# Attention stage of a two-layer diffusion step: TensorE in written order, 18 output products moved into its end

## The chip, the cores and the metric

The kernel runs on one core of a Trainium2 chip. The metric is device time in microseconds (us) of one execution; lower is better. Five engines work side by side and meet only at semaphores: PE (TensorE, matrix products; PEld is its weight load), DVE (VectorE), ACT (ScalarE), POOL (GpSimd) and SP (SyncE, which here only issues transfers). Each engine takes its instructions strictly in the order in which they stand in its queue. An instruction whose data is not there holds up everything behind it on that engine.

## The reference, cut to what matters

Layer 0 is gated grouped-query attention, layer 1 a bidirectional gated recurrence. There are 512 latent tokens and 128 context tokens, width 1024, 16 query heads over 4 key/value heads of 64. Context tokens see only context; latent tokens see context and latent.

```python
h = x * (1.0 + sc) + sh                       # sh, sc, g: three parts of silu(cond) @ ada_w[i] + ada_b[i]
q, k, v, gt = split(h @ w_in)                 # layer 0
q, k = rope(rms_norm(q)), rope(rms_norm(k))
o = softmax(q @ k.T / 8.0) @ v
out = (o * silu(gt)) @ w_out
x = layer_norm(ALPHA * x + g * out)           # then layer 1, of the same frame
```

Everything is float32. Most products are made of three float32r products: each operand is cut into a high and a low part, and high*high, high*low and low*high are summed.

## The kernel before, in words

Tokens go in five tiles of 128 (`TT = 5`: four latent, one context). Layer 0 runs in three stretches: a lead-in (modulation, keys, values, gate, the query heads of group 0), the attention weave, and the output projection with its layer norm (`Norm`, `out_mms`) followed by the transposition for layer 1 (`h1_tile`). Layer 1 fills the second half of the time and its code is not touched.

**The weave.** Two generators take turns. `att_gen` walks over nine units for each key/value group c = 0..3: eight `sample_unit` (one head, 256 latent queries) and one `prompt_unit`. A unit has fronts (scores `sc` in a two-bank PSUM tile, row maximum `nm` on DVE, exponential on ACT, scaling of `p` by POOL) and backs (transposes `pt` of the probabilities, evacuation to `pts` by ACT or DVE); a pair of units ends with the product with the values (`pot`, for the context unit `pscp`, `ptp`, `potp`). Fronts run two units ahead. `Side` hands out everything else, 0.62 of a step (`SIDE_B`) for each step of the attention: the query products `qmm` and their transposes `qps` for the next group (`q_gen`), the modulation products of layer 1 (`ada_gen`, PSUM tile `adaps`), and at the end the weights of the output projection (`wo_gen`) and the split of the gated result (`split_gs`).

**The ring of raw weights.** Every weight block (512 KB) is loaded by SP into one of three `raw` tiles (`rawp`, bufs 3), in the fixed order of the list `order`; `pump` writes the next load when fewer than two (`RAW_AHEAD = 2`) are waiting. A load can start only when the block three places earlier has been used up. Around the attention the list reads: two `attn_w_in` blocks for group c, eight `ada_s` blocks k0..k7, two `attn_w_in` blocks for group c+1, eight more, ...; after the fourth eight come eight `attn_w_out` blocks. An `ada_s` block is used up by four products on PE (`ada_mms` does two blocks at a call: eight products). A block of `attn_w_in` or `attn_w_out` is used up when ACT has cast it (`whi`, `wohi`) and DVE has subtracted (`wlo`, `wolo`).

**What sets the order.** Everything up to the output projection is traced inside `first_half = tc.block(schedule_with_timeline_sim=True)`. There a planner lays out each engine's queue by a timeline of its own: an instruction moves ahead of others of its engine when the planner's timeline says that it is ready sooner. An instruction given to `keep_in_program_order` (`pin`) stays behind the one traced before it on its engine. Loads on SP are pinned; before the change few PE instructions of the attention are.

**PSUM.** The attention has three one-bank tiles (`pt`, `qmm`, `adaps` and others in turn), two two-bank tiles (`sc`, `pscp`) and one bank for `pot`. The output projection opens a new set of four two-bank tiles (`Phase(4, 0)`).

## Time and profile before

| | |
|---|---|
| median of 3 runs | 845.33 us (842.23 to 845.51) |
| the profiled execution: its time | 845.58 us |
| its span, first to last instruction | 843.5 us |
| mean granted TensorE clock | 0.988 of full |
| PE busy | 816.5 us of the span |
| attention weave | from about 140 to 337 us |
| output projection | from 337.0 us |

The span is cut by engine; times in the profile count from the first instruction. A line such as L276 is a line of the kernel before. A chain row gives start, length and what ran; a wait row gives the total, the number of times and the longest. Operations on plain float32 operands show twice as many PE records as products are written: `x16` in the trace is eight `adaps` products.

### The profile page before, as it was taken

Reading aid. Unit: us, or ns where it says so; the run is one execution under the profiler, and the core shown is the slowest. Engines: PE = TensorE matmul, PEld = TensorE weight load, DVE = VectorE, ACT = ScalarE, POOL = GpSimd, SP = SyncE. Lnnn points to the kernel's source line nnn. Section 1 sums busy time; section 2 is a strip of 40 time slices with the busy share of each in tenths; the row PEclk is TensorE's granted clock in tenths of the full one; section 3 lists DMA queues with packets and bytes.
Section 4 is the critical chain, followed back from the end, with each engine's and each line's share of the span. In section 5 each row is a group of like instructions: output and inputs, shape, how many; then the busy total and the mean of one; then the engine's idle time right before and its main releaser. Section 6 shows DMA issues by size and latency. Waiting matters only on the chain.

```text
span 843.5 us, 19410 instructions
## 1 busy us (share of the span) xinstructions
PE 816.5 (97%) x8157; PEld 732.1 (87%) x8157; DVE 532.1 (63%) x954; ACT 380.3 (45%) x769; POOL 213.6 (25%) x263
## 2 busy tenths in 40 slices
PE   8999999989999998999999999999999999999994
PEld 6789999768888766888999999999999999998774
DVE  3675534665557666776438575767668575858476
ACT  2242535563556767222434534435434544445232
POOL 0123001535334743010001304143333314121121
PEclk8999999999999999999999999999999999999997
DMA  9923120145141245630323322331332323314041
GB/s 330 387 86 105 55 72 26 52 162 196 51 157 52 100 133 169 225 125 35 111 66 67 108 68 82 83 108 52 107 89 83 93 67 89 120 65 157 26 157 75
DMA packets 34134, 92.50 MB, mean 110 GB/s; under 512 B 5040, under 2 KB 12224, under 8 KB 34048
## 3 DMA queue, kind: packets, MB, share of 16 engines
q1 hardware_dynamic: 23280, 73.05, 25.9%
q0 software_dynamic: 4864, 14.44, 5.7%
q10 hardware_dynamic: 5904, 3.78, 1.5%
q8 instruction: 64, 1.05, 0.5%
q14 instruction: 22, 0.18, 0.1%
HBM read 82.06 MB, written 9.19 MB: 108 GB/s over the span
## 4 chain that ended last, share of the span: by engine, by line
PE 89%; DVE 5%; ACT 2%; DMA 2%; issue 1%; POOL 1%; SPq 0%; DVEq 0%; ACTq 0%; POOLq 0%
PE rps L1289 7%; PE rps L1290 7%; PE rps L1291 7%; PE vgps L1279 5%; PE vgps L1280 5%; PE vgps L1281 5%; PE pot L868 4%; PE outp L1128 4%; PE pt L954 4%; PE outp L1130 3%; PE outp L1129 3%; PE acc L525 3%; PE lv L1422 2%; PE gps L338 2%; PE gps L340 2%; PE gps L339 2%
## 5 line engine op out<-in xcount | busy, mean ns | idle before, releaser
L1289 PE MATMUL rps<-h1hi,rhi 128*128 128x320 f32 x368 | 118.3, 321 | 0.0
L1290 PE MATMUL rps<-h1lo,rhi 128*128 128x320 f32 x368 | 113.8, 309 | 0.0
L1291 PE MATMUL rps<-h1hi,rlo 128*128 128x320 f32 x368 | 113.6, 309 | 0.0
L947 POOL TENSOR_SCALAR p<-p,rc 128x640 f32<-128x640 f32 x64 | 56.0, 878 | 124.0 <-DVE rc L946 112.7
L1289 PEld LDWEIGHTS rps<-h1hi,rhi 128*128 128x128 f32 x368 | 69.1, 188 | 1.3
L1290 PEld LDWEIGHTS rps<-h1lo,rhi 128*128 128x128 f32 x368 | 69.2, 188 | 0.0
L1291 PEld LDWEIGHTS rps<-h1hi,rlo 128*128 128x128 f32 x368 | 69.1, 188 | 0.0
L233 DVE TENSOR_TENSOR rlo<-raw,rhi 128x1024 fp32r<-128x1024 f32 x32 | 45.1, 1411 | 33.9 <-ACT rhi L232 33.9
L941 ACT ACTIVATE p<-sc,nm 128x640 f32<-128x640 f32 x64 | 51.4, 804 | 31.0 <-DVE nm L936 18.6
L936 DVE TENSOR_REDUCE nm<-sc 128x1 f32<-128x640 f32 x64 | 52.0, 818 | 21.2 <-PE sc L842 21.1
L1450 POOL COPY At<-near 32x160 f32<-32x160 f32 x32 | 14.0, 438 | 195.2 <-DVE near L1412 194.2
L232 ACT CAST rhi<-raw 128x1024 fp32r<-128x1024 f32 x32 | 33.6, 1049 | 51.8 <-PE rps L1290 48.7
L1400 ACT COPY kc<-A 128x640 f32<-128x640 f32 x40 | 32.2, 806 | 54.0 <-DVE A L1431 50.1
L1279 PE MATMUL vgps<-rhi,h1hi 128*128 128x256 f32 x180 | 51.5, 286 | 0.0
L1280 PE MATMUL vgps<-rlo,h1hi 128*128 128x256 f32 x180 | 50.9, 283 | 0.0
L1281 PE MATMUL vgps<-rhi,h1lo 128*128 128x256 f32 x180 | 50.8, 282 | 0.0
L954 PE MATMUL pt<-small,p 128*128 128x128 f32 x320 | 49.6, 279 | 0.8 <-ACT pts L846 0.5
L841 PE MATMUL sc<-kk,X 128*128 128x320 f32 x128 | 42.9, 344 | 5.0 <-ACT p L941 5.0
L954 PEld LDWEIGHTS pt<-small,p 128*128 128x128 f32 x320 | 36.8, 141 | 10.1 <-issue 5.6
L846 ACT COPY pts<-pt 128x512 f32<-128x512 f32 x64 | 36.8, 594 | 17.4 <-PE pt L954 17.3
L1279 PE MATMUL vgps<-wspare,h1hi 128*128 128x256 f32 x140 | 41.7, 298 | 0.0
L338 PE MATMUL gps<-hhi,whi 128*128 128x320 f32 x128 | 40.0, 313 | 0.4 <-ACT X L693 0.4
(298 smaller groups left out, 2393.7 us busy)
## 6 DMA issues: line engine op xcount, KB each, us to landing
raw<-in_rec_w_in SPq DMA_DIRECT2D x40, 512.0 KB, 3.7
raw<-in_ada_s SPq DMA_DIRECT2D x32, 512.0 KB, 4.3
raw<-in_ada_m SPq DMA_DIRECT2D x16, 512.0 KB, 7.9
raw<-in_attn_w_in SPq DMA_DIRECT2D x16, 512.0 KB, 4.6
raw<-in_attn_w_out SPq DMA_DIRECT2D x8, 512.0 KB, 4.3
raw<-in_rec_w_out SPq DMA_DIRECT2D x8, 512.0 KB, 3.9
x1d<-y SPq DMA_DIRECT2D x5, 512.0 KB, 2.6
rx<-x1d POOLq DMA_DIRECT2D x20, 128.0 KB, 3.2
```

The lines of the kernel that those rows point to most:

```text
L233: (lo_eng or nc.gpsimd).tensor_tensor(lo, raw, hi.bitcast(F32), ALU.subtract)
L338: nc.tensor.matmul(ps[:, :320], w.hi(k)[:, c], hhi[:, k, t], start=(k == 0), stop=False)
L936: nc.vector.tensor_reduce(nm[:, 0:1], sc[:, :, :320], AX.XY, ALU.max, negate=True)
L941: return nc.scalar.activation(halves(p[:]), sc[:, :, :320], AF.Exp, bias=nm[:, 0:1], accum_out=su[:, 0:1])
L947: nc.gpsimd.tensor_scalar(p, p, rs[:, 0:1], 1.0, ALU.mult, ALU.mult)
L954: nc.tensor.transpose(pt[:, i * 256 + q * P:i * 256 + (q + 1) * P], ps[q][:, (k0 + i) * P:(k0 + i + 1) * P], ident)
L1279: nc.tensor.matmul(out, h1hi[:, k, t], hi, start=(k == 0), stop=False)
L1280: nc.tensor.matmul(out, h1hi[:, k, t], lo, start=False, stop=False)
L1281: nc.tensor.matmul(out, h1lo[:, k, t], hi, start=False, stop=(k == KT - 1))
L1289: nc.tensor.matmul(ps[:, j, :320], hi[:, k, :], h1hi[:, k, t], start=(k == 0), stop=False)
L1290: nc.tensor.matmul(ps[:, j, :320], hi[:, k, :], h1lo[:, k, t], start=False, stop=False)
L1291: nc.tensor.matmul(ps[:, j, :320], lo[:, k, :], h1hi[:, k, t], start=False, stop=(k == KT - 1))
```

## The change

1. From the end of the lead-in to the end of the attention, every PE instruction (`listed_pe`) is pinned in the order in which the program writes it. All other engines of the block are still ordered by the planner, now around a fixed PE queue. The one `issue_after` that put the first front behind a query product is gone.
2. `early_mms` does 18 of the 24 products of the output projection for token tile 0, columns 0 to 511 (k = 0..5), inside the attention: 6 after the last unit but one, 4 after the last unit, 8 after the last `pot`. Its sum goes through two ACT copies (`part`) to SBUF; two DVE adds put it back. `side.finish()` is called before the first six, so all side work is written ahead of the last two units.
3. Token tiles 1 and 0 share two PSUM tiles, one for each half of the columns, and are done in the order (1, first half), (0, k = 6, 7), (1, second half), (0, second half). The new PSUM set is opened after the planner's block, and its tiles wait only for what lay in their own place (`reuse_waits="tile"`).

```diff
+EARLY_OUT = (6, 4, 8)
-                pools["b2"] = self.st.enter_context(pool("b2", n2, space=PSUM))
+                pools["b2"] = self.st.enter_context(pool("b2", n2, space=PSUM, reuse_waits="tile"))
+    listed = [False]
+    def listed_pe(ins):
+        return pin(ins) if listed[0] else ins
...
-                nc.tensor.matmul(ps[32 * q:32 * q + 32, :CW], sil[:, k, :], raw[:, q * CW:(q + 1) * CW],
-                                 start=(k % 2 == 0), stop=(k % 2 == 1))
+                listed_pe(nc.tensor.matmul(ps[32 * q:32 * q + 32, :CW], sil[:, k, :], raw[:, q * CW:(q + 1) * CW],
+                                           start=(k % 2 == 0), stop=(k % 2 == 1)))
...
+            left_over = len(units) - u
+            if left_over == 2:
+                yield from flush()
...
+            if left_over < 3:
+                early_out(EARLY_OUT[2 - left_over])
+                yield
         yield from flush()
         while later:
             tick()
+        early_out(EARLY_OUT[2])
+        drain(early)
+        listed[0] = False
...
+    def early_mms():
+        ps = bank2("outq")[:, 0, :]
+        t = slice(0, P)
+        for k in range(6):
+            hi, lo = (w[:, k % 2, :] for w in wo[0, k // 2])
+            for x, w in ((hhi, hi), (hhi, lo), (hlo, hi)):
+                yield pin(nc.tensor.matmul(ps, x[:, k, t], w, start=(k == 0 and x is hhi and w is hi),
+                                           stop=(k == 5 and x is hlo)))
+        for n in range(2):
+            part.append(rowp.tile([P, CW], F32, tag="row", name="part"))
+            nc.scalar.copy(part[n], ps[:, n * CW:(n + 1) * CW])
+    early = early_mms()
+    def early_out(n):
+        side.finish()
+        for _ in range(n):
+            next(early)
...
+    listed[0] = True
     for _ in range(3):
         side.step()
-    with tc.issue_after(last_qmm[0]):
-        next(att)
     weave(att, side, SIDE_B)
...
+            if (self.tt, nh) == (0, 0):
+                for n in range(2):
+                    c = slice(n * CW, (n + 1) * CW)
+                    nc.vector.tensor_tensor(y[:, c], self.ps[0][:, c], part[n], ALU.add)
+                nc.vector.tensor_tensor(y, y, g, ALU.mult)
...
-    for tt, nh in ((0, 0), (1, 0), (0, 1), (1, 1), (2, 0), (2, 1), (3, 0), (3, 1), (4, 0), (4, 1)):
...
+    shared = [bank2("outp") for _ in range(2)]
+    for tt in (1, 0):
+        norms[tt] = Norm(tt, [t[:, 1 - tt, :] for t in shared])
+    for nh in range(2):
+        out_mms(norms[1].ps, 1, nh, hhi, hlo)
+        out_mms(norms[0].ps, 0, nh, hhi, hlo, range(0 if nh else 6, KT), first=0 if nh else 6)
```

In the rows below `adaps` is an `ada_s` product (x8: two blocks, x4: one), `qps` a transposition of queries, the rest as above.

**Place 1: PE, where the query work of group 1 ends and that of group 2 begins.** Before, from the block k6 of the second eight to the first block (k0) of the third:

```order
L276 MATMUL adaps<-raw,sil 32x256 x4
L868 MATMUL pot<-pts,vv 64x256 x4
L841 MATMUL sc<-kk,X_1512 128x320
L842 MATMUL sc<-klo,X_1512 128x320
L841 MATMUL sc<-kk,X_1512 128x320
L842 MATMUL sc<-klo,X_1512 128x320
L691 MATMUL qps<-identr,qs_2112 128x128 x4
L954 MATMUL pt<-small,p 128x128 x4
L841 MATMUL sc<-kk,X_1512 128x320
L842 MATMUL sc<-klo,X_1512 128x320
L276 MATMUL adaps<-raw,sil 32x256 x4
```

Now, from k4 and k5 of the one eight to k0 and k1 of the next:

```order
L282 MATMUL adaps<-raw,sil 32x256 x8
L961 MATMUL pt<-small,p 128x128 x2
L847 MATMUL sc<-kk,X_1512 128x320
L848 MATMUL sc<-klo,X_1512 128x320
L847 MATMUL sc<-kk,X_1512 128x320
L848 MATMUL sc<-klo,X_1512 128x320
L282 MATMUL adaps<-raw,sil 32x256 x8
L697 MATMUL qps<-identr,qs_2112 128x128 x4
L961 MATMUL pt<-small,p 128x128 x4
L282 MATMUL adaps<-raw,sil 32x256 x8
```

The planner had cut the calls of two blocks into single blocks with other work between them; now three calls stand close together.

**Place 2: PE in group 3, the last eight `ada_s` blocks.** Before, k3 to k5:

```order
L276 MATMUL adaps<-raw,sil 32x256 x4
L841 MATMUL sc<-kk,X_2860 128x320
L842 MATMUL sc<-klo,X_2860 128x320
L841 MATMUL sc<-kk,X_2860 128x320
L842 MATMUL sc<-klo,X_2860 128x320
L276 MATMUL adaps<-raw,sil 32x256 x4
L954 MATMUL pt<-small,p 128x128 x4
L841 MATMUL sc<-kk,X_2860 128x320
L842 MATMUL sc<-klo,X_2860 128x320
L841 MATMUL sc<-kk,X_2860 128x320
L842 MATMUL sc<-klo,X_2860 128x320
L276 MATMUL adaps<-raw,sil 32x256 x4
```

Now, k0 to k5; after four `sc` and one `pt` x4 follow k6 and k7:

```order
L282 MATMUL adaps<-raw,sil 32x256 x8
L961 MATMUL pt<-small,p 128x128 x4
L847 MATMUL sc<-kk,X_2860 128x320
L848 MATMUL sc<-klo,X_2860 128x320
L847 MATMUL sc<-kk,X_2860 128x320
L848 MATMUL sc<-klo,X_2860 128x320
L282 MATMUL adaps<-raw,sil 32x256 x8
L961 MATMUL pt<-small,p 128x128 x2
L282 MATMUL adaps<-raw,sil 32x256 x8
```

The eight blocks, which were spread over several units, stand within one and a half.

**Place 3: ACT just behind, around the casts of the output weights (`wohi`).** Before:

```order
L898 ACTIVATE pp,sup<-pscp,nmp 128x128 x4
L941 ACTIVATE p,su<-sc,nm 128x640
L846 COPY pts<-pt 128x512
L941 ACTIVATE p,su<-sc,nm 128x640
L846 COPY pts<-pt 128x512
L941 ACTIVATE p,su<-sc,nm 128x640
L232 CAST wohi<-raw 128x1024
```

Now:

```order
L948 ACTIVATE p,su<-sc,nm 128x640
L238 CAST wohi<-raw 128x1024
L852 COPY pts<-pt 128x512
L238 CAST wohi<-raw 128x1024 x2
L852 COPY pts<-pt 128x512 x2
L238 CAST wohi<-raw 128x1024
L905 ACTIVATE pp,sup<-pscp,nmp 128x128 x4
L948 ACTIVATE p,su<-sc,nm 128x640 x2
```

Four casts, each of which needs a loaded block, now stand ahead of the exponentials of the context unit (`pp`); before, those came first.

More of the change, by code (lines that the diff above doesn't have):

```diff
@@ L310, in ada_out @@
         for j in range(2):
-            nc.tensor.transpose(ps[:, j * P:(j + 1) * P], acc[:, j * P:(j + 1) * P], ident)
+            listed_pe(nc.tensor.transpose(ps[:, j * P:(j + 1) * P], acc[:, j * P:(j + 1) * P], ident))
         for j in range(2):
@@ L346, in tok_gen @@
         for k in range(KT):
-            nc.tensor.matmul(out, hhi[:, k, t], w.hi(k), start=(k == 0), stop=False)
-            nc.tensor.matmul(out, hhi[:, k, t], w.lo(k), start=False, stop=False)
-            last_qmm[:] = [nc.tensor.matmul(out, hlo[:, k, t], w.hi(k), start=False, stop=(k == KT - 1)).ins]
+            listed_pe(nc.tensor.matmul(out, hhi[:, k, t], w.hi(k), start=(k == 0), stop=False))
+            listed_pe(nc.tensor.matmul(out, hhi[:, k, t], w.lo(k), start=False, stop=False))
+            last_qmm[:] = [listed_pe(nc.tensor.matmul(out, hlo[:, k, t], w.hi(k), start=False, stop=(k == KT - 1))).ins]
             if k % 4 == 3:
@@ L690, in back @@
                 s = i * 512 + h * P
-                nc.tensor.transpose(pr[:, h * P:(h + 1) * P], s2[:, s:s + P], identr)
+                listed_pe(nc.tensor.transpose(pr[:, h * P:(h + 1) * P], s2[:, s:s + P], identr))
             c0 = (tt0 + i) * P
@@ L840, in score_mms @@
     def score_mms(out, X, c, h, t0, k0, k1):
-        nc.tensor.matmul(out, X[:, h, t0:t0 + P], kk[:, c, k0:k1], start=True, stop=False)
-        nc.tensor.matmul(out, X[:, h, t0:t0 + P], klo[:, c, k0:k1], start=False, stop=True)
+        listed_pe(nc.tensor.matmul(out, X[:, h, t0:t0 + P], kk[:, c, k0:k1], start=True, stop=False))
+        listed_pe(nc.tensor.matmul(out, X[:, h, t0:t0 + P], klo[:, c, k0:k1], start=False, stop=True))
     def keep_pt(ps, w, eng):
@@ L867, in av_mms @@
         for j in (1, 0):
-            nc.tensor.matmul(pot[j * HD:(j + 1) * HD, :CW], vv[:, slot, c * HD:(c + 1) * HD], moving[j], start=first, stop=last)
+            listed_pe(nc.tensor.matmul(pot[j * HD:(j + 1) * HD, :CW], vv[:, slot, c * HD:(c + 1) * HD], moving[j],
+                                       start=first, stop=last))
     def av_out(pot, gt):
@@ L911, in trans @@
                 s = (h % 2 * 2 + h // 2) * P
-                nc.tensor.transpose(pt[:, s:s + P], st["p"][:, h * P:(h + 1) * P], ident)
+                listed_pe(nc.tensor.transpose(pt[:, s:s + P], st["p"][:, h * P:(h + 1) * P], ident))
             st["s"] = keep_pt(pt, 512, nc.scalar.copy)
@@ L953, in trans @@
                 for q in range(2):
-                    nc.tensor.transpose(pt[:, i * 256 + q * P:i * 256 + (q + 1) * P],
-                                        ps[q][:, (k0 + i) * P:(k0 + i + 1) * P], ident)
+                    listed_pe(nc.tensor.transpose(pt[:, i * 256 + q * P:i * 256 + (q + 1) * P],
+                                                  ps[q][:, (k0 + i) * P:(k0 + i + 1) * P], ident))
             pts[k0] = keep_pt(pt, m * 256, nc.scalar.copy if m == 2 else nc.vector.tensor_copy)
@@ L1064, in hybrid_step @@
     wo = {}
+    part = []
+    def early_mms():
[14 more added lines that the diff above has]
+            next(early)
     def wo_gen(layer, pieces, wpool):
@@ L1108, in hybrid_step @@
     right.close()
-    ph = Phase(4, 0)
     h1p = rpool("h1p", 1)
@@ L1120, in bank_of, with out_mms @@
     def bank_of(ps, nh, c):
+        if isinstance(ps, list):
+            return ps[nh][:, c]
         return ps[nh, c.start][:, 0, c] if isinstance(ps, dict) else ps[:, nh, c]
-    def out_mms(ps, tt, nh, ghi, glo, ks=range(KT), c=slice(0, 512)):
+    def out_mms(ps, tt, nh, ghi, glo, ks=range(KT), c=slice(0, 512), first=0):
         t = slice(tt * P, (tt + 1) * P)
@@ L1127, in out_mms @@
             hi, lo = (w[:, k % 2, c] for w in wo[nh, k // 2])
-            nc.tensor.matmul(out, ghi[:, k, t], hi, start=(k == 0), stop=False)
+            nc.tensor.matmul(out, ghi[:, k, t], hi, start=(k == first), stop=False)
             nc.tensor.matmul(out, ghi[:, k, t], lo, start=False, stop=False)
@@ L1132, in hybrid_step, with __init__ @@
     class Norm:
-        def __init__(self, tt):
-            self.tt, self.ps = tt, bank2("outp")
+        def __init__(self, tt, banks=None):
+            if banks is None:
+                both = bank2("outp")
+                banks = [both[:, nh, :] for nh in range(2)]
+            self.tt, self.ps = tt, banks
             self.x = lnp.tile([P, D], F32, tag="x", name="x", bufs=2)
@@ L1143, in half @@
             g = gate[0][:, 1 if self.tt == TS else 0, s]
-            nc.vector.tensor_tensor(y, self.ps[:, nh, :], g, ALU.mult)
+            if (self.tt, nh) == (0, 0):
[3 more added lines that the diff above has]
+                nc.vector.tensor_tensor(y, y, g, ALU.mult)
+            else:
+                nc.vector.tensor_tensor(y, self.ps[nh], g, ALU.mult)
             nc.vector.scalar_tensor_tensor(y, self.x[:, s], ALPHA, y, ALU.mult, ALU.add)
@@ L1218, in hybrid_step @@
     first_half.__exit__(None, None, None)
+    ph = Phase(4, 0)
     h1hi = gsp.tile([P, KT, NT], F32R, tag="gs", name="h1hi")
@@ L1356, in hybrid_step @@
     norms = {}
-    for tt, nh in ((0, 0), (1, 0), (0, 1), (1, 1), (2, 0), (2, 1), (3, 0), (3, 1), (4, 0), (4, 1)):
-        if nh == 0:
-            norms[tt] = Norm(tt)
-        out_mms(norms[tt].ps, tt, nh, hhi, hlo)
-        norms[tt].half(nh)
-        if nh == 1:
-            norms[tt].finish()
-            if tt > 1:
-                h1_tile(tt - 1, norms[tt - 1].y)
-            elif tt == 1:
-                h1_tile(0, norms[0].y)
+    shared = [bank2("outp") for _ in range(2)]
[4 more added lines that the diff above has]
+        out_mms(norms[0].ps, 0, nh, hhi, hlo, range(0 if nh else 6, KT), first=0 if nh else 6)
+        for tt in (1, 0):
+            norms[tt].half(nh)
+            if nh:
+                norms[tt].finish()
+    for tt in range(2, TT):
+        norms[tt] = Norm(tt)
+        out_mms(norms[tt].ps, tt, 0, hhi, hlo)
+        if tt == 2:
+            h1_tile(1, norms[1].y)
+        norms[tt].half(0)
+        out_mms(norms[tt].ps, tt, 1, hhi, hlo)
+        norms[tt].half(1)
+        norms[tt].finish()
+        h1_tile(0 if tt == 2 else tt - 1, norms[0 if tt == 2 else tt - 1].y)
     for _ in range(4):
```

## The prediction

> **What bounds the kernel now.** First the page: span, PE, and the chain that ended last by engine.

> ```profile
> span 843.5 us, 19410 instructions
> PE 816.5 (97%) x8157; PEld 732.1 (87%) x8157; DVE 532.1 (63%) x954; ACT 380.3 (45%) x769; POOL 213.6 (25%) x263
> PE 89%; DVE 5%; ACT 2%; DMA 2%; issue 1%; POOL 1%; SPq 0%; DVEq 0%; ACTq 0%; POOLq 0%
> ```

> PE is the chain. An order can win only PE's idle time, and loses whatever new idle time it makes. So next the windows of the attention: start:end, length, busy time of PE, PEld, DVE, ACT, POOL, then granted clock, DMA share, GB/s.

> ```profile
> 140.00:337.00 197.00, 189.29 (x1601) 150.09 (x1599) 125.61 (x283) 121.69 (x274) 87.82 (x94) 0.99 0.34 115
> 179.30:194.40 15.10, 13.04 (x110) 8.37 (x109) 8.79 (x15) 7.07 (x15) 8.12 (x12) 0.89 0.70 229
> 302.00:318.00 16.00, 15.52 (x146) 10.20 (x145) 10.28 (x24) 9.30 (x25) 7.28 (x9) 1.00 0.63 208
> 318.00:329.00 11.00, 10.02 (x78) 7.83 (x76) 9.51 (x16) 10.29 (x20) 5.21 (x8) 1.00 0.70 225
> 329.00:337.00 8.00, 6.80 (x57) 4.41 (x57) 3.29 (x9) 3.91 (x9) 2.18 (x2) 1.00 0.23 69
> 337.00:360.00 23.00, 23.00 (x105) 19.15 (x106) 15.90 (x22) 6.38 (x7) 2.27 (x4) 1.00 0.65 226
> ```

> PE idles 197.00 - 189.29 = 7.71 us in the whole attention, and not at all behind it. That is all there is to win. The idle time lies at 179 to 194 (2.06), 302 to 318 (0.48), 318 to 329 (0.98), 329 to 337 (1.20); 2.99 is spread. Who is waited for (total, times, longest):

> ```profile
> PE sc L841 <- ACT p L941: 5.0, 8, 1.7
> PE adaps L276 <- DMA raw<-in_ada_s: 0.7, 2, 0.4
> PE outp L1128 <- DVE gs L873: 0.5, 1, 0.5
> PE pot L868 <- DVE pts L846: 0.5, 1, 0.5
> ```

> PE almost never waits for the `ada_s` blocks. SP does, for PE:

> ```profile
> SPq L213 <- PE adaps L276: 149.4, 19, 20.0
> ```

> Loads are held by the ring: each goes out only when the block three places earlier is used up. What one takes (min, median, max), near 179 us and near 302 us, with the casts that free a weight block:

> ```profile
> L232 ACT CAST whi<-raw x2: 1046/1050/1054, 185.1 to 187.8; 128x1024 fp32r<-128x1024 f32 x2
> L233 DVE TENSOR_TENSOR wlo<-raw,whi x2: 1225/1456/1687, 186.2 to 189.6; 128x1024 fp32r<-128x1024 f32 x2
> DMA to landing us min/median/max: 3.2/4.1/7.5
> ```
> ```profile
> L232 ACT CAST wohi<-raw x4: 1047/1063/1082, 318.7 to 325.8; 128x1024 fp32r<-128x1024 f32 x4
> L233 DVE TENSOR_TENSOR wolo<-raw,wohi x4: 1211/1278/1336, 319.8 to 326.9; 128x1024 fp32r<-128x1024 f32 x4
> DMA to landing us min/median/max: 3.6/4.3/5.2
> ```

> A load (over 3 us) is longer than most stretches of PE work between two `adaps` calls. Before, the planner spread the blocks. Prices of the pieces, from the chain:

> ```profile
> 179.34 1.00 PE adaps L276 x16
> ...
> 184.16 0.30 PE qps L691 x4
> 184.45 0.46 PE pt L954 x4
> ...
> 193.96 0.57 PE adaps L276 x8
> ...
> 302.38 0.15 PE sc L841
> ...
> 302.97 0.87 PE pt L954 x8
> ...
> 307.15 0.06 PE pscp L841
> ...
> 308.00 2.31 PE pot L868 x20
> ...
> 337.96 0.23 PE outp L1128
> ```

> So: two `ada_s` blocks 1.0 (0.5 each), four `sc` 0.59 (302.97 - 302.38), a `pt` 0.11, four `qps` 0.30, `pscp` 0.85, a whole `pot` 2.31, an output product 0.23.

> **The change, part by part.**

> *A, end of group 1 (place 1).* Count from the start of k4. k5 is read at 1.0; in its place goes the first block of group 2's weights: landed 1.0 + 4.1 = 5.1, cast 6.15, subtracted 7.6; only then may the new k1 be loaded: 11.7, read by 12.2. The other branch is shorter: k4 read 0.5, k7 lands 4.6, read 5.1, new k0 lands 9.2. PE has in its list until there three calls (3.0), two `pt`, four `sc`, `qps` and four `pt`: 4.6. Behind them stand the `pot` and the queries of group 2, and PE cannot reach them. Stall 12.2 - 4.6 = 7.6; with 3.2 and the shortest subtraction 10.2 - 4.6 = 5.6; with 5.2 and the longest 14.6 - 4.6 = 10.0. The 2.06 idle there goes: +5.5 [3.5, 7.9].

> [...]

> *Group 2 to 3.* Between its k6 and k7 and the next k0 PE has sixteen `sc`, twenty `pt` and `qps`: 4 x 0.59 + 20 x 0.11 + 0.30 = 4.9, more than the 4.1 of k0's load; the weight block ahead of k1 was loaded early, since the call of k5 stands a unit further up. 0, and 1.5 at most in E. In group 1 before place 1 the calls stand a unit or more apart.

> *B, the last eight blocks (place 2).* From the start of k0, three blocks being loaded: k0, k1 read 0.5, 1.0; `pt` x4 and `sc` to 2.03; k2 read 2.53; k3 (loaded from 0.5) lands 4.8, read 5.3; `pt` x2; k4 read 6.02; k5 (from 2.53) lands 6.83, read 7.33; `sc`, `pt` to 8.36; k6 (from 5.3) lands 9.6, read 10.1; k7 (from 6.02) lands 10.32, read 10.82. PE's own work is 6.28. Stall 4.5; with 3.6 a load 3.1, with 5.2 6.3. Less 0.48 idle there: +4.0 [2.6, 5.8].

> *C, the casts (place 3).* How ACT stands when its cast waits:

> ```profile
> ACT whi L232 <- DMA raw<-in_attn_w_in: 4.9, 2, 3.8
> ```
> ```profile
> L846 ACT COPY pts<-pt 128x512 f32<-128x512 f32 x64 | 36.8, 594 | 17.4 <-PE pt L954 17.3
> L898 ACT ACTIVATE pp<-pscp,nmp 128x128 f32<-128x128 f32 x16 | 5.7, 372 | 4.3 <-DVE nmp L894 2.9 <-DVE rs_t L188 1.4
> ```

> It held ACT for 3.8 us once before. Count from Z, the end of k7 (10.82 above). The first `attn_w_out` block takes k5's place: lands Z + 0.8, cast 1.9, subtracted 3.15; the fourth block goes in its place and lands 7.45. Second and third land 3.6 and 4.3, casts end 4.65 and 5.7, two `pts` 6.9, fourth cast 8.5, four `pp` 10.0. On PE stand `pt`, `pot`, `pscp`, `pt` x10, `sc`, `pt` x2: 5.5, then an `sc` whose PSUM tile is the one that `pp` reads. Stall 4.5; none if the blocks come sooner than all rows say, 5.4 with 5.2 a load. Less 0.98 idle: +3.5 [-1.0, 4.4].

> *D, the 18 products.* 18 x 0.23 = 4.1 us leave the output projection and enter the attention: nothing by themselves. They stand where PE idles 1.20 (waits for `pts`, `gs`); I take 0.7 of it as filled: -0.7 [-1.2, 0]. ACT's two copies and DVE's two adds lie beside 23.00 busy us of PE at 337 to 360, where DVE has 7.1 free and ACT 16.6: nothing. The second half's weights are due after 30 products, 6.9 us, not 48, 11.0. Their last cast before began here:

> ```profile
> 344.50 1.05 ACT L232 CAST wohi<-raw 128x1024 fp32r<-128x1024 f32 x1 [4.28 <-DMA raw<-in_attn_w_out]
> ```

> Cast and subtraction end near 346.8; PE now wants that block at 337.0 + 6.9 + 18 x 0.23 = 348.0. Covered by 1.2, and the blocks are freed earlier in the list now. POOL issues four loads of `x` ahead of the first `rstdl` (the fourth waits for tile 0's second half), and DVE now does the second halves of tiles 1 and 0 together.

> ```profile
> L1144 DVE TENSOR_TENSOR y<-outp,gate 128x512 f32<-128x512 f32 x10 | 6.9, 686 | 4.0 <-PE outp L1130 4.0
> L189 POOL TENSOR_TENSOR rstdl<-rs_t,mhalf 128x1 f32<-128x1 f32 x5 | 2.8, 563 | 24.0 <-DVE rs_t L188 24.0
> ```

> Six such steps and a `rstdl`, 6 x 0.69 + 0.56 = 4.7 and two short ones, against tile 2's first half on PE, 24 x 0.23 = 5.5, behind which tile 1 is due: 0 [0, 0.6]. The PSUM tiles by place take waits away and add none: PE has none there.

> *E, the rest.* 2.99 idle, mostly `sc` behind ACT; written order can cure or double it: 0 [-3.0, 3.0], since fill stands between fronts in groups 1 and 2 and is missing in 3.

> *F, the clock.*

> ```profile
> 186.20:189.60 3.40, 1.34 (x10) 0.82 (x12) 3.09 (x6) 3.40 (x7) 1.60 (x3) 0.90 0.68 206
> 189.60:193.00 3.40, 3.40 (x24) 2.81 (x17) 1.73 (x3) 0.59 (x1) 3.19 (x5) 0.59 0.75 252
> ```

> Behind a stretch in which PE was busy for 1.34 of 3.40 us, the granted clock is 0.59; over 179.3 to 194.4 that is a loss of (1 - 0.89) x 15.1 = 1.7. A has this already; B and C may each bring one: 0 [-1.7, 3.4]. [...]

> Sum: 5.5 + 4.0 + 3.5 - 0.7 = +12.3. Against the profiled execution 845.58 + 12.3 = 857.9; the median of the runs is 0.25 lower, so 857.6.

> **Rivals.**
> - *The written order cures the waits.* All 5.0 us of `sc` behind ACT and 0.7 of D go: 839.6. For it speaks that `sc` stands evenly between fill. It decides only if a block lands within the PE work between the reading of one block and the use of that three later: in place 1, 1.3 to 1.8 us; the shortest load is 3.2. Chance 0.07.
> - *Stalls pay for waits.* While PE waits for blocks, ACT and DVE empty their queues, so E's 2.99 goes and C never comes; A and B are at their short ends: 3.5 + 2.6 - 1.0 - 0.7 - 3.0 = +1.4, 846.7. Against it: in C it is ACT that is held. Chance 0.13.
> - *The clock falls too*, twice 1.7: 861.0. For it the rows above; against it, stalls in B are cut by calls of 0.5 and 1.0. Chance 0.20.

> **How the numbers follow.** The forecast has 0.60. Corners of all terms at once (-0.8, +25.1) are unlikely; three terms short, or the second rival, give 847 to 849; A, B long with the clock, 867. Range 848 to 867 leaves out the first rival and most of the second, less than 0.2 with the top. About 0.5%, 4.2 us, is what a measurement of this kernel can tell from no change: faster 0.07, same 0.13, slower 0.80.

> **What would show it.** PE waits for `raw<-in_ada_s` should rise from 0.7 to about 10 us, in two places; ACT waits for `attn_w_out`; PE `sc` behind ACT stays near 5, with a single wait over 3 us behind `pp`. The attention's end, 18 products out, comes some 12 us later, and from there the length is as before. I am wrong if blocks land sooner, or if the waits for ACT vanish.

## The result

The change made the kernel slower: 871.54 us median of 4 runs (869.66 to 873.12) against 843.88 (842.23 to 845.51) of the kernel before on the same chip, a ratio of 1.0322 with a 95% interval of 1.0301 to 1.0344. That is +27.7 us where +12.3 was forecast; the range ended at 867. The direction was right, the size was not.

The profiled execution took 873.12 us. Its page, the rows that answer to the first three of before (new line numbers: `adaps` L282, `sc` L847, `pt` L961, `pot` L874, casts L238):

```profile
span 871.3 us, 19420 instructions
PE 823.1 (94%) x8157; PEld 734.1 (84%) x8157; DVE 533.6 (61%) x956; ACT 381.6 (44%) x771; POOL 210.0 (24%) x263
PE 83%; DVE 5%; ACT 3%; DMA 3%; issue 2%; POOL 2%; SPq 0%; DVEq 0%; ACTq 0%; POOLq 0%
```

PE's share of the chain fell from 89% to 83%, and PE is also busy for longer: 823.1 and not 816.5, for the same work. The windows of the changed kernel (columns as in the prediction), the whole attention with its 18 products first, then the three places:

```profile
140.00:367.60 227.60, 200.89 (x1618) 157.09 (x1618) 128.12 (x284) 123.81 (x275) 85.59 (x95) 0.95 0.28 99
179.30:192.60 13.30, 6.71 (x54) 3.21 (x54) 5.16 (x10) 5.45 (x10) 6.07 (x10) 0.74 0.78 267
308.00:330.00 22.00, 17.85 (x152) 12.02 (x150) 10.33 (x24) 10.10 (x23) 7.06 (x8) 0.92 0.39 137
330.00:350.00 20.00, 14.88 (x104) 10.34 (x96) 10.41 (x18) 10.73 (x24) 5.46 (x8) 0.83 0.47 166
```

The attention ends at 367.6; before it ended at 337.0, and with 18 products more it would have ended at 341.1. That is +26.5 us. Idle time of PE is 227.60 - 200.89 = 26.7 us where before had 7.7: +19.0. The rest is in PE's busy time. Behind the attention the remaining output products run from 367.7 to 423.1, as forecast but for one wait of 0.79 us. For whom PE waits between 100 and 400 us:

```profile
PE adaps L282 <- DMA raw<-in_ada_s: 9.4, 6, 3.2
PE sc L847 <- ACT p L948: 6.0, 7, 2.6
PE pt L961 <- ACT pts L852: 3.7, 4, 1.7
PE sc L847 <- ACT pp L905: 2.4, 1, 2.4
PE pt L961 <- POOL p L954: 1.2, 2, 0.8
PE ptp L919 <- POOL pp L911: 1.0, 1, 1.0
```

The long waits stand where the prediction had put them. From the timeline of PE (start, length, what ran, in brackets the idle time ahead of it and who ended it), place 1, place 2 and place 3:

```profile
182.23 0.64 PE L282 MATMUL adaps<-raw,sil 128*32 128x256 f32 x8 [1.60 <-DMA raw<-in_ada_s]
187.03 1.08 PE L282 MATMUL adaps<-raw,sil 128*32 128x256 f32 x8 [3.24 <-DMA raw<-in_ada_s]
...
322.82 0.64 PE L282 MATMUL adaps<-raw,sil 128*32 128x256 f32 x8 [1.14 <-DMA raw<-in_ada_s]
324.28 0.64 PE L282 MATMUL adaps<-raw,sil 128*32 128x256 f32 x8 [0.45 <-DMA raw<-in_ada_s]
326.14 1.08 PE L282 MATMUL adaps<-raw,sil 128*32 128x256 f32 x8 [1.23 <-DMA raw<-in_ada_s]
...
337.67 0.44 PE L961 MATMUL pt<-small,p 128*128 128x128 f32 x2 [1.68 <-ACT pts L852]
340.50 0.64 PE L847 MATMUL sc<-kk,X 128*128 128x320 f32 x1 [2.40 <-ACT pp L905]
342.99 1.11 PE L919 MATMUL ptp<-small,pp 128*128 128x128 f32 x4 [1.05 <-POOL pp L911]
```

With a third wait of 1.75 at place 1 these are 6.6, 2.8 and 5.1 us: 14.5 of the 26.7. The other 12.2 are spread, where before had 2.99 and the 1.20 ahead of the output projection. The lengths also show a clock: the same four `adaps` products (eight records) take 0.64 in one row and 1.08 in another; the granted clock is 1.00 from 182.0 to 182.9 and 0.50 from 186.9 to 188.2. And PE did not pass the late blocks by: the `pt` behind the last two ran at 190.87, though POOL had done the `p` that it reads by 183.11 (182.31 + 0.80).

### The profile page after: what moved, and what is told of

Read it like the earlier page. It is cut to its first block, busy times and chain, and to the rows that moved or that the text cites. A ratio compares the mean times of both kernels' runs of the same rounds, so it can differ in the third digit from the quotient of the medians.

```text
span 871.3 us, 19420 instructions
## 1 busy us (share of the span) xinstructions
PE 823.1 (94%) x8157; PEld 734.1 (84%) x8157; DVE 533.6 (61%) x956; ACT 381.6 (44%) x771; POOL 210.0 (24%) x263
## 3 DMA queue, kind: packets, MB, share of 16 engines
q8 instruction: 64, 1.05, 0.5%
## 4 chain that ended last, share of the span: by engine, by line
PE 83%; DVE 5%; ACT 3%; DMA 3%; issue 2%; POOL 2%; SPq 0%; DVEq 0%; ACTq 0%; POOLq 0%
PE rps L1335 7%; PE rps L1336 6%; PE rps L1337 6%; PE vgps L1325 5%; PE vgps L1327 4%; PE vgps L1326 4%; PE pot L874 4%; PE pt L961 3%; PE outp L1164 3%; PE acc L531 3%; PE outp L1166 3%; PE outp L1165 3%; PE lv L1477 2%; PE gps L344 2%; PE gps L346 2%; PE gps L345 2%
## 5 line engine op out<-in xcount | busy, mean ns | idle before, releaser
L954 POOL TENSOR_SCALAR p<-p,rc 128x640 f32<-128x640 f32 x64 | 53.7, 841 | 149.4 <-DVE rc L953 138.7
L948 ACT ACTIVATE p<-sc,nm 128x640 f32<-128x640 f32 x64 | 51.1, 799 | 51.1 <-DVE nm L943 48.2
L238 ACT CAST rhi<-raw 128x1024 fp32r<-128x1024 f32 x32 | 33.6, 1049 | 52.7 <-PE rps L1336 49.0
L961 PE MATMUL pt<-small,p 128*128 128x128 f32 x320 | 50.5, 284 | 6.4 <-ACT pts L852 3.7
L847 PE MATMUL sc<-kk,X 128*128 128x320 f32 x128 | 43.2, 347 | 8.4 <-ACT p L948 6.0
L961 PEld LDWEIGHTS pt<-small,p 128*128 128x128 f32 x320 | 38.0, 144 | 14.3 <-issue 5.5
L874 PE MATMUL pot<-pts,vv 128*64 128x256 f32 x320 | 41.1, 407 | 0.4 <-DVE pts L852 0.4
```

Source lines behind the costliest of these rows:

```text
L874: listed_pe(nc.tensor.matmul(pot[j * HD:(j + 1) * HD, :CW], vv[:, slot, c * HD:(c + 1) * HD], moving[j], start=first, stop=last))
L948: return nc.scalar.activation(halves(p[:]), sc[:, :, :320], AF.Exp, bias=nm[:, 0:1], accum_out=su[:, 0:1])
L954: nc.gpsimd.tensor_scalar(p, p, rs[:, 0:1], 1.0, ALU.mult, ALU.mult)
L961: listed_pe(nc.tensor.transpose(pt[:, i * 256 + q * P:i * 256 + (q + 1) * P], ps[q][:, (k0 + i) * P:(k0 + i + 1) * P], ident))
```

## The experiments

Each kernel was run beside the kernel before on the same chip. Beside the median the table has the length of the weave in the profiled execution: from the last gate product (`gps`) of the lead-in to the first product of the output projection that is not one of the 18 (4.1 us added for the two kernels without them). This length leaves out the lead-in, which ended anywhere between 131.7 and 135.3 us in the 18 profiles, with no pattern by edit. The medians of the kernel before that stand beside these kernels run from 843.88 to 845.41, so two medians of different rows can be compared to about 1.5 us.

| kernel | what differs from the changed kernel | median us | ratio to before [95%] | weave us | over before |
|---|---|---|---|---|---|
| before | | 843.88 | | 206.2 | |
| after | | 871.54 | 1.0322 [1.0301, 1.0344] | 232.9 | +26.7 |
| end_only | order left to the planner, new end kept | 843.75 | 0.9999 [0.9981, 1.0017] | 205.9 | -0.3 |
| order_only | old end, listed order | 872.32 | 1.0327 [1.0289, 1.0364] | 234.5 | +28.3 |
| ada_free | `ada_s` products off the list | 864.09 | 1.0245 [1.0196, 1.0293] | 225.7 | +19.5 |
| ring4 | a fourth raw tile | 861.15 | 1.0197 [1.0170, 1.0223] | 223.0 | +16.8 |
| warm | 72 idle products in the stalls | 866.01 | 1.0257 [1.0242, 1.0273] | 228.8 | +22.6 |
| sc_free | scores off the list | 853.14 | 1.0105 [1.0084, 1.0125] | 213.8 | +7.6 |
| ada_sc_free | both off | 850.01 | 1.0066 [1.0047, 1.0085] | 211.1 | +4.9 |
| end_ring4 | planner's order, new end, fourth raw tile | 844.16 | 0.9996 [0.9986, 1.0006] | 205.7 | -0.5 |
| sc_ada | only scores and `ada_s` listed | 855.75 | 1.0127 [1.0097, 1.0156] | 216.4 | +10.2 |
| sc_pt | only scores, `pt`, `ptp`, `pot` listed | 865.51 | 1.0236 [1.0204, 1.0268] | 226.5 | +20.3 |
| sc_free_ring4 | scores off, fourth raw tile | 846.40 | 1.0015 [0.9998, 1.0033] | 206.1 | -0.1 |
| lead3 | fronts three units ahead | 869.39 | 1.0294 [1.0276, 1.0311] | 231.2 | +25.0 |
| lead3_ring4 | the same, fourth raw tile | 861.77 | 1.0193 [1.0167, 1.0220] | 221.2 | +15.0 |
| lead3_free_ring4 | planner's order, three units, fourth tile | 846.99 | 1.0028 [1.0012, 1.0044] | 206.4 | +0.2 |
| sc_free_01 | scores of groups 0 and 1 off the list | 869.89 | 1.0297 [1.0252, 1.0342] | 228.4 | +22.2 |
| sc_free_23 | scores of groups 2 and 3 off the list | 857.91 | 1.0164 [1.0128, 1.0200] | 219.5 | +13.3 |

**Which part of the change costs?** `end_only` turns the list off; `order_only` is the kernel before with the listed order.

```diff
-    listed[0] = True
+    listed[0] = False
```

> The changed kernel with the planner free again to order PE in the attention; the 18 early products, the shared PSUM tiles and the new order of the output projection stay. If the written order alone costs the 27.7 us (blocks or fronts), this is within 2 us of the kernel before, 842 to 846. If the end has a part in the loss, it is above 848.

> The kernel before with PE in written order to the end of the attention, and nothing of the new end. If the written order is the whole loss: 869 to 874. If the end costs part of it: below 866.

The order is the whole loss, and the new end is worth nothing either way. `end_only` has the same PE work in its attention as the changed kernel, and so gives the length that this work needs:

```profile
140.00:341.20 201.20, 193.22 (x1622) 154.20 (x1621) 125.86 (x284) 123.47 (x275) 89.89 (x96) 0.99 0.33 112
```

PE is busy for 193.22 us here and for 200.89 in the changed kernel: 7.7 us of the loss are PE being slow, at a granted clock of 0.95 and not 0.99.

**Is it the blocks?** `ada_free` takes the `ada_s` products out of the list: the listed products now follow one another by a chain of their own, and what is off the list is the planner's.

```diff
     def listed_pe(ins):
-        return pin(ins) if listed[0] else ins
+        if listed[0]:
+            if last_listed[0] is None:
+                pin(ins)
+            else:
+                tc.add_manual_dep(ins.ins, last_listed[0],
+                                  mybir.DependencyInfo(mybir.DependencyClass.NoSync, mybir.DependencyReason.DATA),
+                                  reason="listed order")
+            last_listed[0] = ins.ins.name
+        return ins
...
-                listed_pe(nc.tensor.matmul(ps[32 * q:32 * q + 32, :CW], sil[:, k, :], raw[:, q * CW:(q + 1) * CW],
+                nc.tensor.matmul(ps[32 * q:32 * q + 32, :CW], sil[:, k, :], raw[:, q * CW:(q + 1) * CW],
```

`ring4` keeps the list and gives the `ada_s` and `attn_w_in` blocks a fourth raw tile, whose space comes from one probability tile.

```diff
-            raw = (raw0 if start else rawp).tile([P, 1024], F32, tag="raw", name="raw")
+            ring = raw0 if start else rawp
+            if wide:
+                nraw[0] += 1
+                ring = extra[0] if nraw[0] % 4 == 0 else rawp
+            raw = ring.tile([P, 1024], F32, tag="raw", name="raw")
...
-    probs.append((sm, 4))
+    probs.append((sm, 3))
+    extra.append(rpool("rawx", 1))
```

> The changed kernel with the ada_s products taken off the list, so that the planner may place them between the other PE instructions, which keep the written order. Theory 'blocks' (PE waits for loads in place 1 and 2, and the clock falls behind these waits): the 9.4 us of waits for ada_s and about half of the lost clock go, 857 to 861. Theory 'fronts' (scores stand where ACT, DVE and POOL cannot follow): 866 to 870.

> The changed kernel with a fourth raw tile for the ada_s and attn_w_in blocks (three may wait instead of two; one tile fewer for the probabilities makes room). The order on PE is the same. Theory 'blocks': the waits for ada_s fall from 9.4 to 3 to 5 us, and the time to 862 to 867. Theory 'fronts': 869 to 873.

`ada_free` fell between its two expectations (its four runs lie far apart, 861.99 to 871.03); `ring4` came out a little better than the theory that favoured it. The waits did not follow that theory: PE still waits for `ada_s` blocks for 7.8 us in `ada_free`, though the planner may now place them, and for 6.3 us in `ring4`, where 3 to 5 were expected. Loads are a cause all the same: 10.4 us go with one more tile. They are not the only one, since 17 us stay.

**Is it the clock?** `warm` fills part of the stalls with products that nothing reads; the planner also put a few ACT casts otherwise around them, which matters at place 3 (below).

```diff
+WARM_UP = {(0, 7): 12, (1, 0): 24, (1, 1): 12, (3, 3): 8, (3, 5): 8, (3, 7): 8}
...
+            n = WARM_UP.get((sup, k), 0)
+            hot = pop[0].tile([P, 512], F32, tag="po", name="hot") if n else None
+            for _ in range(n):
+                listed_pe(nc.tensor.matmul(hot[:, :CW], kk[:, 0, :P], kk[:, 0, :CW], start=True, stop=True))
```

> The changed kernel with 72 extra products of 128x256 whose results are not used, put into PE's list ahead of the `ada_s` calls that wait: 12 ahead of k7 of group 1's blocks, 24 and 12 ahead of the next two, 8 ahead of three of the last eight. They fill time in which PE stands still and make no transfer sooner. Clock theory (part of the loss is the granted clock that falls behind each stall, about 7.5 us of PE busy time above what before needed): the granted clock in 180 to 200 and 340 to 360 rises from 0.74 and 0.85 to above 0.9, and the time is 864 to 867. Rival (the time is set by the waits alone, and a slow clock beside them costs nothing): the clock rises and the time stays at 870 to 874.

The time came out as the clock theory had it, 866.0. First the changed kernel, from 180 to 200 and 340 to 350, and its `pot` behind place 1; then `warm` from 180 to 200, 340 to 360 and the same `pot`:

```profile
180.00:200.00 20.00, 13.41 (x96) 8.18 (x96) 5.61 (x10) 5.27 (x10) 5.37 (x10) 0.74 0.75 267
340.00:350.00 10.00, 8.45 (x48) 5.82 (x48) 4.50 (x10) 3.47 (x11) 2.61 (x3) 0.69 0.30 105
...
191.92 4.38 PE L874 MATMUL pot<-pts,vv 128*64 128x256 f32 x20
```
```profile
180.00:200.00 20.00, 19.45 (x168) 16.65 (x160) 6.52 (x11) 6.99 (x12) 5.70 (x10) 1.00 0.66 219
340.00:360.00 20.00, 18.11 (x129) 13.53 (x126) 9.68 (x21) 10.79 (x22) 5.16 (x7) 1.00 0.01 2
...
188.21 2.38 PE L879 MATMUL pot<-pts,vv 128*64 128x256 f32 x20
```

One `pot` (twenty records, ten products) takes 4.38 us behind the stall (granted clock 0.53 from 191.9 to 196.3) and 2.38 when PE was kept busy (1.00 from 186.2 to 192.0 of `warm`). By the medians 5.5 us came back, by the weave 4.1. Not all of that need be the clock: at place 3 of `warm` the planner puts the fourth cast behind `pp`, and the three waits there are 0.49, 1.45 and 1.27 us, 1.9 less than in the changed kernel. Nor is the clock cured: in `warm` it is 0.91 from 240 to 260 and 0.96 from 300 to 340; place 3 lies ahead of 340 there.

**Is it the scores?** `sc_free` takes the score products off the list, `ada_sc_free` those and the `ada_s` products, by the same chain as above.

```diff
-        listed_pe(nc.tensor.matmul(out, X[:, h, t0:t0 + P], kk[:, c, k0:k1], start=True, stop=False))
-        listed_pe(nc.tensor.matmul(out, X[:, h, t0:t0 + P], klo[:, c, k0:k1], start=False, stop=True))
+        nc.tensor.matmul(out, X[:, h, t0:t0 + P], kk[:, c, k0:k1], start=True, stop=False)
+        nc.tensor.matmul(out, X[:, h, t0:t0 + P], klo[:, c, k0:k1], start=False, stop=True)
```

> The changed kernel with the score products (`sc`, `pscp`) left to the planner, everything else of PE's order held to the list. Fronts theory (scores stand where ScalarE, VectorE and GpSimd cannot follow, and this is the larger part of the 12 us of spread idle time): PE's waits for `p` and `pp` fall by 6 us or more, and the time is 858 to 864. Blocks theory (the idle time and the clock come from the loads that the three raw tiles hold back): 868 or more, with the waits for `ada_s` blocks still 8 to 10 us.

> The changed kernel with both the `ada_s` products and the score products left to the planner; `pt`, `pot`, the queries and the out-projection products stay in the listed order. If the two causes are separate and together are the loss: 848 to 854, with PE's waits for blocks and for `p` near those of before (0.7 and 5.0 us). If the places of `pt` and `pot` carry a cost of their own: above 856.

This is the largest single effect, larger than expected: 18.4 of the 27.7 us come back, though `ada_s` stays listed. PE's waits for `p` and `pp` fall from 8.4 to 3.1 us, a little less than the 6 that were asked for. PE's busy time is nearly back with it (the lead-in ended 1.1 us earlier here, so the window begins that much further on in the work):

```profile
140.00:347.40 207.40, 193.28 (x1610) 152.53 (x1609) 127.51 (x283) 122.39 (x275) 87.91 (x95) 0.98 0.32 109
```

Freeing the blocks too adds only 3.1 us, where alone it gave 7.4; both free, 5.6 us over the kernel before of its group stay. Place 1 is not cured in `sc_free`. Its three long waits there, and one score ahead of the third:

```profile
181.76 0.64 PE L292 MATMUL adaps<-raw,sil 128*32 128x256 f32 x8 [1.23 <-DMA raw<-in_ada_s]
187.24 0.64 PE L292 MATMUL adaps<-raw,sil 128*32 128x256 f32 x8 [2.07 <-DVE wlo L249]
187.81 0.42 PE L857 MATMUL sc<-kk,X 128*128 128x320 f32 x1
191.24 1.08 PE L292 MATMUL adaps<-raw,sil 128*32 128x256 f32 x8 [2.58 <-DMA raw<-in_ada_s]
```

PE waits for 5.9 us there, where it was 6.6 with the scores listed. What is gone is idle time behind: the first row below is the changed kernel, the second `sc_free`, each from 260 us to the end of its attention.

```profile
260.00:367.70 107.70, 93.66 (x734) 70.70 (x733) 59.93 (x130) 62.19 (x136) 44.23 (x48) 0.95 0.25 89
```
```profile
260.00:347.40 87.40, 83.45 (x682) 63.57 (x682) 55.32 (x121) 57.98 (x127) 43.58 (x46) 1.00 0.31 107
```

**What are the scores held by?** `sc_ada` lists only the scores and the `ada_s` products, `sc_pt` only the scores and the products of the softmax tiles; the others read `pass_on(...)` in place of `listed_pe(...)`.

> Only the score products and the `ada_s` products are held to the list, against each other; `pt`, `pot`, the queries and their weights' products are the planner's. Theory "scores behind blocks" (what costs most is that no score can pass a block that PE waits for, so that PE, ScalarE and VectorE all run dry there): 856 to 864, most of the 18.4 us that freeing the scores gave back. Theory "scores between pt" (what costs is the place of the scores among `pt` and `pot`, where the list paces them by ScalarE's copies): 844 to 850.

> Only the score products and the products of the softmax tiles (`pt`, `ptp`, `pot`) are held to the list, against each other; the `ada_s` blocks, the queries and their weights' products are the planner's. Theory "scores between pt": 856 to 864. Theory "scores behind blocks": 844 to 850.

Both ties cost: +10.3 us and +20.1, each over the kernel before of its group, and the place among `pt` and `pot` is the heavier one. `sc_pt` also holds `pt` and `pot` against each other, so not all of its 20.1 need be the scores'; `ada_free`, which lists the queries as well, is +20.1 too. The two theories had been put as a choice, and that was wrong; the sum of both, 30, is more than the 27.7 of the whole list, so they pay for the same idle time in part. In `sc_pt` PE waits for 8.8 us on `ada_s` blocks that are not listed at all:

```profile
PE adaps L292 <- DMA raw<-in_ada_s: 8.8, 6, 4.4
```

A block's call stalls PE there although the planner was free to put other work ahead of it; the likely reading is that, with the scores tied to `pt`, there was less to put there.

**Do loads and scores make up the whole?** `sc_free_ring4` joins the two edits.

> The listed order with the score products left to the planner, and a fourth raw tile for the `ada_s` and `attn_w_in` blocks. If the 9 us that are left with free scores come from the loads behind three raw tiles: 844 to 848, with PE's waits for `ada_s` below 2 us (7.0 with three tiles, 2.1 of them for the tile's release). If they come from the listed place of `pt`, `pot` and the queries: 850 to 853.

Yes: 846.4, +1.0 over the kernel before, and the interval of the ratio takes in 1; PE's waits for `ada_s` are down to 0.4 us. All else of PE's attention is still in the written order, and with four tiles that costs nothing that can be measured; with three, `ada_sc_free` stayed at +5.6. In medians over the kernel before of each group:

| | three raw tiles | four |
|---|---|---|
| scores listed | +27.7 | +17.1 |
| scores free | +8.7 | +1.0 |

So the scores' place is worth 19.0 with three tiles and 16.1 with four, the tile 10.6 and 7.7.

**Is it the distance?** In PE's queues one can count how many score tiles stand ahead at the first `pt` of each tile. In the kernel before the mean is 4.4; in the list it is 4 and 3 by turns, falling to 2 and 1 at each context unit, mean 3.2; in `sc_free` mean 4.8. (These are counts of the queues as built; in the traces, where some `pt` records are missing, the kernels stand in the same order, but the means can't be read exactly.) `lead3` writes the fronts three units ahead (mean 4.8, never under 3 before the last two units), `lead3_ring4` adds the fourth tile.

```diff
-        AHEAD = 2
+        AHEAD = 3
```

> The changed kernel with the fronts written three units ahead and not two: at the first `pt` of a score tile, 4.8 tiles' scores stand ahead in PE's list on average (4.5 to 5.5), where the changed kernel has 3.2 (3.0 to 3.5) and the kernel before has 4.4. Theory "short lead" (the list fixes how far the scores run ahead, and 3 tiles are used up whenever PE, a cast or a block stands still): ScalarE's wait for the maxima falls from 48 us to below 30, and the time is 853 to 862. Rival (it is the adapting of the scores to the moment that counts, not their distance): 866 or more, ScalarE's wait above 40.

> The same longer lead with the fourth raw tile: the two causes of the listed order's loss both treated, PE's order still wholly the list's. If short lead and held loads are together the cause: 844 to 851 (ring4 alone is 861.2). If the list costs by itself: 856 or more.

The theory of the short lead fell: 869.4, and with four tiles 861.8 where two units ahead gave 861.2. ACT's wait for the maxima stayed high. In the kernel before, in the changed kernel, in `lead3` and, for comparison, in `sc_free`:

```profile
ACT p L941 <- DVE nm L936: 18.6, 16, 3.2
```
```profile
ACT p L948 <- DVE nm L943: 48.2, 26, 6.9
```
```profile
ACT p L948 <- DVE nm L943: 44.4, 23, 4.9
PE adaps L282 <- DMA raw<-in_ada_s: 12.5, 7, 3.1
```
```profile
ACT p L958 <- DVE nm L953: 13.1, 14, 2.8
```

The test is not quite clean, since the side work is handed out by steps of the attention and so the blocks moved too: PE's wait for them rose from 9.4 to 12.5.

**Where do the scores matter?** `sc_free_01` and `sc_free_23` free one half of the groups each.

```diff
+        hold = listed_pe if c < 2 else pass_on
+        hold(nc.tensor.matmul(out, X[:, h, t0:t0 + P], kk[:, c, k0:k1], start=True, stop=False))
```

> The changed kernel with the scores of groups 0 and 1 left to the planner (they may rise into the stall at place 1; up to 8 tiles ahead of their `pt`), those of groups 2 and 3 listed. Local theory (each stall costs what its own group's scores could have filled): 865 to 869, since the larger part of the idle time lies behind 244 us, in groups 2 and 3. Carried theory (scores done early in the stall at place 1 give a lead that lasts through the later groups): 861 or less.

> The changed kernel with the scores of groups 2 and 3 left to the planner, among them those of the context unit of group 3 that stood behind the last `ada_s` blocks and behind the casts of the output weights; those of groups 0 and 1 listed. Local theory: 856 to 861, with the idle time between 300 and 360 us mostly gone. Carried theory: 866 or more.

It is mostly local. Groups 2 and 3 give back 13.6 us; groups 0 and 1 give 1.7, within the intervals (4.5 by the weave, but the profiled execution was one of the quicker of runs from 864.90 to 872.27). A lead gathered at place 1 (up to 8 tiles in `sc_free_01`) isn't carried on. What the free scores do in group 3 is plain on ACT. The context unit's exponentials (`pp`) and the casts of the output weights, first in the changed kernel, then in `sc_free_23`:

```profile
331.57 1.05 ACT L238 CAST wohi<-raw 128x1024 fp32r<-128x1024 f32 x1 [0.81 <-DMA raw<-in_attn_w_out]
334.76 1.05 ACT L238 CAST wohi<-raw 128x1024 fp32r<-128x1024 f32 x1 [1.65 <-DMA raw<-in_attn_w_out]
336.08 1.04 ACT L238 CAST wohi<-raw 128x1024 fp32r<-128x1024 f32 x1 [0.28 <-DMA raw<-in_attn_w_out]
...
338.93 0.38 ACT L905 ACTIVATE pp<-pscp,nmp 128x128 f32<-128x128 f32 x1
```
```profile
318.92 0.37 ACT L916 ACTIVATE pp<-pscp,nmp 128x128 f32<-128x128 f32 x1 [1.66 <-DVE rc L964]
325.20 1.05 ACT L248 CAST wohi<-raw 128x1024 fp32r<-128x1024 f32 x1
```

In the list the context unit's scores stand behind all eight blocks; free, they stand between the blocks, and their exponentials are done by 320.4, 4.8 us before the first cast.

**A version better than both?** `end_ring4` is `end_only` with the fourth tile; `lead3_free_ring4` has three units ahead as well.

> The planner's order with the new end of the attention (18 early products, PSUM tiles shared by halves) and a fourth raw tile for the `ada_s` and `attn_w_in` blocks. If the stall at 179 to 194 us of the kernel before (2.06 us idle and about 1.7 us of lost clock) comes from the three raw tiles: 838 to 842. If it has another cause: 842.5 to 845.5, no different from before.

> The planner's order with the new end, the fourth raw tile and fronts three units ahead (mean lead 4.6 tiles). If the lead is what the fourth raw tile left short (3.6 tiles there, 844.2): 838 to 842. If the planner has no idle time left that a lead can cover: 842.5 to 846.

Neither beats the kernel before; the second is 2.8 us slower. The stall at 179 to 194 us did go: from 180 to 200 PE of `end_ring4` is busy for 19.07 us at full clock, where the kernel before has 17.94 at 0.91. Yet its weave is only 0.5 shorter than that of the kernel before, and 0.2 shorter than that of `end_only`, from which it differs by the fourth tile alone:

```profile
180.00:200.00 20.00, 19.07 (x174) 14.96 (x167) 12.56 (x26) 10.50 (x20) 10.62 (x13) 1.00 0.85 310
300.00:340.00 40.00, 36.98 (x286) 25.33 (x286) 22.83 (x47) 25.26 (x55) 15.36 (x21) 0.96 0.44 146
...
PE ptp L925 <- ACT pts L858: 2.1, 1, 2.1
```

A new wait of 2.1 for ACT and a dip of the clock to 0.96 stand in group 3. The saved time came back there as other waits.

## Why the prediction was wrong in size

- *A, place 1.* Forecast 7.6 idle, +5.5 net of before. Measured 1.60 + 3.24 + 1.75 = 6.6, so +4.5. The mechanism was right, the size within its range.
- *B, the last eight blocks.* Forecast 4.5, +4.0 net; measured 2.8, +2.3, a little under the lower bound of 2.6.
- *C, the casts.* Forecast 4.5, +3.5 net; measured 1.68 + 2.40 + 1.05 = 5.1, +4.1, behind the casts as described, though in three waits and not in the single one over 3 us that was named as the sign. But the same mechanism stood at a second place, which step "group 2 to 3" had put at 0: it counted enough PE work to cover the blocks of `ada_s` and did not look at the casts on ACT. From ACT's timeline, and PE's:

```profile
244.16 1.04 ACT L238 CAST whi<-raw 128x1024 fp32r<-128x1024 f32 x1 [0.91 <-DMA raw<-in_attn_w_in]
245.11 0.58 ACT L852 COPY pts<-pt 128x512 f32<-128x512 f32 x1
245.58 0.80 ACT L948 ACTIVATE p<-sc,nm 128x640 f32<-128x640 f32 x1
```
```profile
246.53 0.42 PE L847 MATMUL sc<-kk,X 128*128 128x320 f32 x1 [2.62 <-ACT p L948]
```

- *D, the 18 products.* Forecast -0.7 with the fill of 1.20 idle us; `end_only` shows 0 (-0.3 in the weave). Behind the attention the new wait of 0.79 us is a little over the 0.6 that was allowed for.
- *E, the rest of the attention, the step that failed.* Forecast 0 [-3, 3] for idle time spread between fronts. Of PE's 26.7 idle us 12.2 lie outside A, B and C; the same stretches had 2.99 + 1.20 before: +8.0 with D. There PE's waits for `p` went from 2.4 to 6.0 us (2.62 of them behind the cast just shown) and those of `pt` for `pts` from 0.5 to 2.0. Each stall was counted as time that PE loses once. But the scores that stand behind it in the list are also what ACT, DVE and POOL live on: ACT's wait for the maxima rose from 18.6 to 48.2 us. The reading is that these engines ran dry with PE and the next fronts had to be done one after the other, where the planner had put scores into such gaps; no run shows this chain by itself. What `sc_free` does show is that it hangs on the scores: with them free, 5.9 us of idle time are left outside A, B and C, 6.3 less, and ACT's wait is 13.1. The rest of what `sc_free` gave is 3.9 us at C, 1.7 at B, 0.7 at A and some 6.6 of clock. `sc_free_23` shows where.
- *F, the clock, the other step that was mis-sized.* Forecast 0 [-1.7, 3.4]; measured 200.89 - 193.22 = +7.7. The clock fell behind four groups of stalls, not one or two (last section).

A, B and C together gave +11.0 where +13.0 was forecast; D with E +8.0 where -0.7 was; F +7.7 where 0 was. The sum is +26.7 against 26.5 in the attention (F is 7.5 if the 193.4 us stand for the need that before's 189.29 and the 18 products of 0.23 make). E and F both lie above their ranges, so far that the measured +27.7 is more than the +25.1 that the prediction had with all its terms at their upper ends. The rival "stalls pay for waits" had the sign of E wrong: PE's waits for exponentials rose, from 5.0 us in all to 6.0, and 8.4 with those for `pp`. The rival "the clock falls too" had the right term with less than half its size (3.4 of 7.7); what the prediction set against it, that calls cut the stalls of B, did not keep the clock up there: 0.50 for 3.4 us from 325.7. What stays open is which property of the planner's place for the scores does it. It is not the mean distance alone, and it is mostly local to the half of the groups that was freed; more was not tried.

## What to carry to other kernels

Price a stall in a fixed order three times: its own length (here +11.0 us at A, B and C), what the engines downstream lack because their producer stands behind it (the reading of the +8.0 of D with E), and the slow clock that follows (+7.7). Before an order is fixed, compare in the old and new queues where the products that feed other engines (here the scores) stand around each late load and each cast that waits for one, and leave those free first: with them free and one more raw tile, all else of the written order cost +1.0 us with an interval that takes in none. An order that was laid around waits can hide them: when one was taken away here (`end_ring4`), others came in its place.

## What was not expected of the hardware

```profile
182.40:185.80 3.40, 1.39 (x16) 0.75 (x8) 0.81 (x2) 2.34 (x4) 2.82 (x5) 1.00 0.88 319
185.80:196.00 10.20, 7.22 (x40) 3.35 (x40) 2.40 (x3) 1.30 (x2) 1.65 (x3) 0.50 0.79 271
336.00:339.40 3.40, 0.44 (x2) 0.20 (x2) 3.40 (x6) 3.32 (x7) 0.00 (x0) 1.00 0.52 193
339.40:346.20 6.80, 4.65 (x18) 2.99 (x20) 3.38 (x8) 3.29 (x12) 2.61 (x3) 0.50 0.47 163
```

All four lengths are about 3.4 us or two or three times that, and in the 3.4 us ahead of the four falls PE was busy for 1.39, 0.78, 1.65 and 0.44 us. In the 3.4 us from 179.0, with a wait of 1.60 us, it was busy for 1.80, and the clock stayed at 1.00 for the next 3.4. So the longest wait does not tell these stretches apart: at place 2 waits of 1.14, 0.45 and 1.23 us in a row came with a fall, the 1.60 by itself with none. The busy time of the 3.4 us ahead does tell these five apart, but five rows place no line.

The price is the second surprise: 7.7 us in an attention of 228. It can be counted a second way. PE was busy for 7.22, 3.40, 2.96 and 4.65 us in the four slow stretches, 18.2 in all; if a product takes twice as long at 0.50, an estimate (`pot` took 4.38 us and not 2.38, 1.84 times as long), half of that, 9.1, is lost. `end_only` has a granted clock of 0.97 from 140 to 200 and of 1.00 behind, and loses about (1 - 0.97) x 60 = 1.8, so 7.3 are the list's. Idle products in the stalls, which do nothing else, gave back 4.1 to 5.5, with the doubt about 1.9 of it that place 3 of `warm` leaves.
